# One two-layer decoder step on one core: value stores on another queue, quarter sums and pooling sums spread over the stages, projections interleaved

## The chip, the cores and the metric

One NeuronCore of a Trainium2 chip; the other cores are idle. The metric is the device time of one launch in microseconds. A core has TensorE (matmuls, PE in the profile; PEld is its weight load), VectorE (DVE), ScalarE (ACT), GpSimd (POOL) and SyncE (SP), which here only issues DMAs. Each engine runs its own instructions in the order in which they were issued to it, and waits at its head for whatever that instruction needs. Matmul results land in PSUM, all other tiles are in SBUF, inputs and outputs in HBM.

## What is computed

A trunk of two layers over 1024 prompt tokens and 8 sample tokens, 1024 features, float32. Cut to what matters here:

```python
h = x @ w_in[l]                       # columns: pooling, gating MLP, queries, keys, values, gates
q, k = rope(q), rope(k)               # 8 query heads, 2 key heads of 64
ya = pool_mix(xa) * silu(za)          # causal means over 2, 4, 8, 16 tokens
vn = layer_norm(v_sgu, sg, sb)        # the gating MLP's values, normalised
yb = u * sgu_spatial(vn) * silu(zb)
yc = window_attention(q, k, v, sinks) * silu(zc)
y  = sum(sigmoid(g_i) * (y_i @ w_proj_i) for i in (a, b, c))
x  = layer_norm(ALPHA * x + y @ w_out[l])
```

Key, value, pooling and gating states are outputs too.

## The kernel before

**Arithmetic.** A float32 product is three matmuls on a faster input type: each operand is split into a high and a low half (`split`, L96: a ScalarE copy L97 makes the high half, a subtraction L98 the low half, on VectorE unless GpSimd is named), and h*xh + h*xl + lo*xh is summed in PSUM. The input x lies transposed in SBUF as XH and XL, 8 tiles of 128 features by 1032 tokens; HT = 516 tokens are half of it.

**Weights** come in through SyncE's queue in the order of `order()` into six raw buffers `wr` (L92). The list `todo` holds the preparations in that order; `prep()` runs the next one, which splits one half tile of weights (512 columns) into `wh` and `wl` (four buffers each), puts it on the list `ready` and issues further loads.

**Stages of a layer**, the times of the first layer in brackets:

- Values (`a0`, 0 to 60): nine blocks of tokens, 24 matmuls each over values and gating values. `a0_post` (L347) copies the values on ScalarE, and normalises the gating values: statistics on VectorE, a power on GpSimd (L304), subtract and multiply on VectorE (L357), then scale and bias as two GpSimd operations (L358, L359). The stores of these rows are issued on ScalarE's queue, one block late.
- Rotation (`rope`, 60 to 120): five column tiles (keys, four of queries) of three units (matmuls L607). Each unit copies four quarters on ScalarE (L387), multiplies on VectorE (L388, L389) and adds on GpSimd (L390). After the keys a job `keys_out` transposes the last ones (L398) for the output, eight pumps later.
- Gates (`gates`, 120 to 450, twelve calls of `pair`, L847): a pair computes 2 x 2 quarter results with seven products (`product`, L832, matmuls L839) of sums of weights with sums of input quarters, like Strassen's. VectorE adds a product to the results (L855, L865), which frees its PSUM buffers. Sums of weights are made on GpSimd (L209 to L217), quarter sums of the input (`S`, L672 to L702) and their splits (`P`, into T2x, T3x, T4x) by jobs during the value and rotation stages (`queue_folds`). Attention runs as jobs in between: `att_scores` (L457), `att_norm` (L479), transposes (L496), weighted sums.
- Pooling branch (450 to 500): `pool_sums` (L749) doubles running sums on GpSimd, further jobs widen them on VectorE (L772).
- Gating MLP, then the last gated branch `gate_c` (to 569), whose result is finished by L917 to L919. The branches' results are split as yh, yl by `split_y` and `split_c`, four of these eight low halves on GpSimd.
- Projections (`project(d)`, from 569, matmuls L964): for each of eight column tiles d three groups i (pooling and gating MLP: two feature tiles each; attention: four). VectorE multiplies each half group by its gate out of PSUM (L969); gates were stored to HBM and are loaded again (L942).
- Output projection, layer norm and transposes (to 772), then the second layer, whose value and rotation stage lies at 772 to 890.

**Jobs.** Class `Jobs` keeps four lists. Stages call `pump()`: one call is one tick, and runs the jobs whose conditions hold. A condition is a pair (event, lag): the job may start that many ticks after the event. Of list 3, the quarter sums, one job at most starts per pump. `need(event)` runs whatever is missing for an event at once.

PSUM has eight buffers: four `acc` (value, rotation, products, half of the projections) and four `att`.

Of the kernel before, what the change touches and what calls it, by code (L numbers as in the profile page):

```python
# [18 lines left out]
S = 1024  # L19
# [82 lines left out]
def trunk_kernel(  # L102
# [69 lines left out]
    def order():  # L172
        for l in range(L):
# [160 lines left out]
    class Layer:  # L334
        def __init__(self, l):
            self.l, self.c, self.jobs = l, LC[l], Jobs()
            self.s, self.pt, self.res, self.rr, self.row, self.y = [{} for _ in range(6)]
            self.late, self.step, self.vn_out = deque(), 0, None
# [8 lines left out]
        def a0_post(self, b, p):  # L347
# [9 lines left out]
            V.tensor_scalar(vn_dst[:n], p[:n, 128:384], mv[:n, 0:1], mv[:n, 1:2], op0=ALU.subtract, op1=ALU.mult)  # L357
            G.tensor_tensor(vn_dst[:n], vn_dst[:n], c["sg"][:n], op=ALU.mult)  # L358
            G.tensor_tensor(vn_dst[:n], vn_dst[:n], c["sb"][:n], op=ALU.add)  # L359
            if self.vn_out:  # L360
                self.vn_out()
                self.vn_out = None
            if b < NB:
                self.vn_out = lambda: A.dma_start(out=vnd[:, b], in_=vn_dst)
            if b == NB - 1:
                A.dma_start(out=vp_o[l], in_=v_dst)
            elif b == NB:
                A.dma_start(out=vs_o[l, :, 127, :], in_=self.vs)
                A.dma_start(out=cv_o[l], in_=vn_dst[:NS])
                A.dma_start(out=vnsd, in_=vn_dst[:NS])  # L370
# [86 lines left out]
        def att_scores(self, q):  # L457
# [3 lines left out]
            st, nm, su = self.s[q] = (t_ap()[:, 0:512], *self.two(t_sm(4, "ns")))  # L461
# [14 lines left out]
            V.tensor_tensor(nm, nm, self.c["sk"][:, j:j + 2], op=ALU.add)  # L476
            A.activation(nm, nm, AF.Exp)
# [198 lines left out]
        def queue_folds(self):  # L676
# [32 lines left out]
            prev = [("x", 1)]  # L709
# [6 lines left out]
            def P_(n, k, *at):  # L716
                nonlocal prev
                J.add(3, lambda: parts(n, k), ("TT", n, k), prev + list(at))
                prev = [(("TT", n, k), 1)]
# [29 lines left out]
        def pool_sums(self, j):  # L749
# [4 lines left out]
            G.tensor_tensor(X[:, 1:S], x[:, 1:S], x[:, 0:S - 1], op=ALU.add)  # L754
            G.tensor_copy(X[:, 0:1], x[:, 0:1])
# [6 lines left out]
            self.jobs.mark(("sum", j))  # L762
            nxt, J = Y if cur is X else X, self.jobs
# [68 lines left out]
        def product(self, n, ps, first):  # L832
            h, lo = ready.popleft()
            for k in range(4):
# [9 lines left out]
                if k in (0, 2) and len(ready) < 3:  # L844
                    prep()
# [87 lines left out]
        def open_gates(self):  # L933
            self.g = {}

        def load_gate(self, i, d, q):
            if d < 8:
                n = i or d % 2 * 3
                if n not in self.g:
                    self.g[n] = t_u(("u4", "u5", "u6", "u7")[n], [T], F32, "gl")  # L940
                e = slice(q * HT, q * HT + HT)
                SP.dma_start(out=self.g[n][:, e], in_=gd[i][d][:, e])  # L942
# [6 lines left out]
        def project(self, d):  # L949
            w = ready.popleft(), ready.popleft()  # L950
            m = self.g[d % 2 * 3]
            last = d == 7
            for i in range(3):
                t = self.g[i] if i else m
# [354 lines left out]
```

## Time and profile before

| | before |
|---|---|
| median of 3 runs | 1545.0 us (1543.7 to 1545.22) |
| the profiled execution, its own time | 1546.7 us |
| its span, first to last instruction | 1545.0 us |
| mean granted clock of TensorE | 0.979 of full speed |
| busy: TensorE, VectorE | 1468.7 us (95%), 1035.1 us (67%) |
| busy: ScalarE, GpSimd | 611.4 us (40%), 540.0 us (35%) |
| DMA, mean over the span | 98 GB/s |

Busy time counts computing instructions only. Rows of a timeline give the start, the duration, the engine, the line of the kernel and its tiles, and in brackets how long the engine stood idle before and what ended it.

### The profile page before, as it was taken

How to read it: one execution, taken by the hardware profiler on the slowest of the kernel's cores; microseconds unless marked ns; L12 is line 12 of the kernel's file. 1: busy time of each engine (PE TensorE's matmuls, PEld its weight loads, DVE VectorE, ACT ScalarE, POOL GpSimd, SP SyncE). 2: the span in 40 equal slices, each digit the busy share in tenths (PEclk: the TensorE clock that was granted, in tenths of full speed). 3: DMA queues.
4: the chain of work that ended last, by engine and by line, in shares of the span. 5: the costliest groups of instructions: out<-in, count | busy, mean ns of one | idle time of the engine just before them, and what ended most of it. 6: DMA issues, size and time to landing. Idle time of an engine off the chain costs nothing. (4 is left out here: it accounts for less than half of the span.)

```text
span 1545.0 us, 27806 instructions
## 1 busy us (share of the span) xinstructions
PE 1468.7 (95%) x10592; PEld 1379.1 (89%) x10592; DVE 1035.1 (67%) x2262; ACT 611.4 (40%) x1419; POOL 540.0 (35%) x520
## 2 busy tenths in 40 slices
PE   8898999999999999999997989999999999899998
PEld 8788999999999989988796989999999999899886
DVE  6785666666558686654888756666766586866547
ACT  4365555565532242220213645655555332422200
POOL 4534322332143124510574443232312422245015
PEclk9999999999999998999998999999999999999999
DMA  7312222222222125642323121222222221256413
GB/s 250 109 43 68 71 83 83 77 89 76 90 80 73 49 76 173 210 144 93 136 75 119 51 69 63 97 69 84 82 84 83 88 71 46 85 186 205 132 49 123
DMA packets 82388, 151.92 MB, mean 98 GB/s; under 512 B 13216, under 2 KB 22512, under 8 KB 82224
## 3 DMA queue, kind: packets, MB, share of 16 engines
q1 hardware_dynamic: 62928, 113.65, 23.7%
q10 hardware_dynamic: 19328, 36.51, 6.2%
q8 instruction: 83, 1.36, 0.4%
q14 instruction: 49, 0.40, 0.1%
HBM read 113.62 MB, written 38.58 MB: 99 GB/s over the span
## 5 line engine op out<-in xcount | busy, mean ns | idle before, releaser
L839 PE MATMUL acc<-XH,wh 128*128 128x258 f32 x1152 | 235.9, 286 | 3.9 <-ACT gu L865 3.4
L839 PE MATMUL acc<-XL,wh 128*128 128x258 f32 x1152 | 235.4, 286 | 0.0
L839 PE MATMUL acc<-XH,wl 128*128 128x258 f32 x1152 | 235.2, 285 | 0.0
L98 DVE TENSOR_TENSOR wl<-wr,wh 128x512 fp32r<-128x512 f32 x196 | 155.2, 792 | 94.8 <-ACT wh L97 90.7
L839 PEld LDWEIGHTS acc<-XH,wh 128*128 128x128 f32 x1152 | 178.9, 189 | 9.8 <-issue 4.2
L839 PEld LDWEIGHTS acc<-XH,wl 128*128 128x128 f32 x1152 | 178.7, 189 | 5.5 <-issue 5.0
L839 PEld LDWEIGHTS acc<-XL,wh 128*128 128x128 f32 x1152 | 178.6, 189 | 4.7 <-issue 4.2
L97 ACT ACTIVATE wh<-wr 128x512 fp32r<-128x512 f32 x196 | 122.1, 624 | 131.9 <-PE acc L839 42.5
L210 POOL TENSOR_TENSOR st<-st,wr 128x512 f32<-128x512 f32 x36 | 51.5, 1430 | 287.2 <-DVE wl L98 244.5
L98 DVE TENSOR_TENSOR wl<-st,wh 128x512 fp32r<-128x512 f32 x108 | 85.2, 789 | 68.6 <-ACT wh L97 67.1
L315 PE MATMUL acc<-slx,XH 128*128 128x512 f32 (+1 forms) x384 | 113.4, 377 | 0.4 <-DVE slx L98 0.4
L839 PE MATMUL acc<-T2x,wh 128*128 128x258 f32 x576 | 101.6, 294 | 10.8 <-DVE gu L855 10.8
L971 POOL TENSOR_TENSOR glu<-glu,glu 128x516 f32<-128x516 f32 x56 | 80.5, 1449 | 83.1 <-DVE glu L969 45.1
L474 ACT ACTIVATE ap<-ap,ns 128x256 f32<-128x256 f32 (+1 forms) x128 | 62.4, 488 | 113.1 <-DVE ns L472 113.1
L855 DVE TENSOR_TENSOR gu<-gu,acc 128x258 f32<-128x258 f32 x240 | 90.0, 416 | 18.4 <-PE acc L839 18.4
L839 PE MATMUL acc<-T4x,wh 128*128 128x258 f32 x576 | 99.0, 294 | 3.3 <-DVE zyu L855 3.3
L905 ACT ACTIVATE gu<-gu,halves 128x258 f32<-128x258 f32 x144 | 65.7, 504 | 90.8 <-DVE gu L855 89.2
L839 PE MATMUL acc<-T3x,wh 128*128 128x258 f32 x576 | 98.1, 288 | 0.9 <-DVE gu L855 0.9
L839 PEld LDWEIGHTS acc<-T2x,wh 128*128 128x128 f32 x576 | 83.3, 194 | 16.2 <-issue 9.9
L217 POOL TENSOR_TENSOR st<-wr,st 128x512 f32<-128x512 f32 x36 | 48.3, 1342 | 130.9 <-issue 127.8
L607 PE MATMUL acc<-XH,wh 128*128 128x384 f32 (+1 forms) x240 | 80.8, 337 | 10.6 <-DVE kTu L388 5.5
L209 POOL TENSOR_TENSOR st<-wr 128x512 f32<-128x512 f32 x36 | 47.2, 1312 | 123.6 <-DVE wl L98 88.5
(252 smaller groups left out, 3583.0 us busy)
## 6 DMA issues: line engine op xcount, KB each, us to landing
wr<-in_wS_dram SPq DMA_DIRECT2D x144, 256.0 KB, 2.6
gd<-gu ACTq DMA_DIRECT2D x48, 516.0 KB, 2.7
glu<-gd SPq DMA_DIRECT2D x96, 258.0 KB, 2.7
wr<-in_wP_dram SPq DMA_DIRECT2D x32, 256.0 KB
wr<-in_wO_dram SPq DMA_DIRECT2D x32, 256.0 KB, 3.4
wr<-in_wB_dram SPq DMA_DIRECT2D x20, 256.0 KB, 2.7
w<-in_xp_dram SPq DMA_DIRECT2D x16, 256.0 KB
w<-x2d SPq DMA_DIRECT2D x16, 256.0 KB, 2.6
```

Of the source, the lines that this page charges most:

```text
L97: nc.scalar.activation(h, raw, AF.Copy)
L98: (eng or nc.vector).tensor_tensor(lo, raw, h.bitcast(F32), op=ALU.subtract)
L209: G.tensor_tensor(s1[:, 0:512], a21, a22, op=ALU.add)
L210: G.tensor_tensor(s2[:, 0:512], s1[:, 0:512], a11, op=ALU.subtract)
L217: G.tensor_tensor(s4[:, 0:512], a12, sums[p][1], op=ALU.subtract)
L315: PE.matmul(p[:, 0:n], x[:, k, blk(b)], c, start=(i == 0 and j == 0), stop=(i == len(terms) - 1 and j == len(t) - 1))
L474: A.activation(o, o, AF.Exp, bias=nm[:, i:i + 1], scale=-1.0, accum_out=su[:, i:i + 1])
L607: PE.matmul(p[:, 0:n], a[:, c], b[:, k, o:o + n], start=(k == 0 and j == 0), stop=(k == 7 and j == 2))
L839: PE.matmul(ps[s][:, 0:258], a[:, c], b[:, s * 258:s * 258 + 258], start=(first and k == 0 and j == 0), stop=(k == 3 and j == 2), skip_gro ...
L855: V.tensor_tensor(part(c, q, s), part(*a, s), b[s][:, 0:258], op=ALU.add)
L905: A.activation(o, p, AF.Tanh, bias=self.c["h"][:, i * 8 + d + c:i * 8 + d + c + 1], scale=0.5)
L971: (V if last else G).tensor_tensor(m[:, e], m[:, e], t[:, e], op=ALU.add)
```

## The change

1. `order()`: the weight halves of the first two projection tiles come by half, not by tile.
2. `a0_post`: normalise, scale and bias as two VectorE operations, none on GpSimd; the stores of these rows are issued on SyncE's queue, at the next block (`send`).
3. `keys_out` 16 pumps after the keys, not 8.
4. `att_scores`: the sink term of the softmax gets a result tile of its own (`sn`), where it overwrote the negative maximum.
5. `queue_folds`: other lags between the quarter sums. The last split P(4,3) moves in the first layer from tick 80 to 91, in the second from 65 to 78, of 96.
6. `pool_sums`: the doublings are jobs of list 3, four pumps apart, where they were issued in one go.
7. `product`: the two weight preparations come after matmul groups 1 and 5, ahead of the pumps at 3 and 7, where they came at the end of tiles 0 and 2.
8. `project`: the first two column tiles are interleaved (pooling of both, gating MLP of both, then attention of both); gates are loaded by this order; the splits of yc go between the first groups, and all low halves are VectorE's.
9. `split_x`, first layer: the low halves of input blocks 3, 5 and 7 on GpSimd.

```diff
 order():
-            for d in range(8):
+            yield from [wP[l, d, :, h * 512:h * 512 + 512] for h in range(2) for d in range(2)]
+            for d in range(2, 8):
 a0_post():
-            V.tensor_scalar(vn_dst[:n], p[:n, 128:384], mv[:n, 0:1], mv[:n, 1:2], op0=ALU.subtract, op1=ALU.mult)
-            G.tensor_tensor(vn_dst[:n], vn_dst[:n], c["sg"][:n], op=ALU.mult)
-            G.tensor_tensor(vn_dst[:n], vn_dst[:n], c["sb"][:n], op=ALU.add)
-            if self.vn_out:
-                self.vn_out()
+            V.scalar_tensor_tensor(vn, p[:n, 128:384], mv[:n, 0:1], c["sg"][:n], op0=ALU.subtract, op1=ALU.mult)
+            V.scalar_tensor_tensor(vn, vn, mv[:n, 1:2], c["sb"][:n], op0=ALU.mult, op1=ALU.add)
+            self.send()
...
+        def send(self):
+            for dst, src in self.out:
+                SP.dma_start(out=dst, in_=src)
+            self.out = []
 rope():
+                if s == 1:
+                    self.send()
-                self.jobs.add(0, self.keys_out, None, [("k", 8)])
+                self.jobs.add(0, self.keys_out, None, [("k", 16)])
 att_scores():
-            V.tensor_tensor(nm, nm, self.c["sk"][:, j:j + 2], op=ALU.add)
-            A.activation(nm, nm, AF.Exp)
+            V.tensor_tensor(sn, nm, self.c["sk"][:, j:j + 2], op=ALU.add)
+            A.activation(sn, sn, AF.Exp)
 queue_folds():
+            prev, gap = [("x", 1)], 1 + self.l
-                prev = [(("TT", n, k), 1)]
+                prev = [(("TT", n, k), gap)]
-            S_(2, 0, 3, ("wA", 1))
+            S_(2, 0, 3, ("wA", 2))
+            lag = 4 - self.l
-                S_(4, k, 2)
+                S_(4, k, lag)
-                    S_(2, k + 1, 3)
+                    S_(2, k + 1, lag)
 pool_sums():
+            def double(a, b, sh):
+                G.tensor_tensor(b[:, sh:S], a[:, sh:S], a[:, 0:S - sh], op=ALU.add)
+                G.tensor_copy(b[:, 0:sh], a[:, 0:sh])
+                return False
...
-                G.tensor_tensor(nxt[:, sh:S], cur[:, sh:S], cur[:, 0:S - sh], op=ALU.add)
-                G.tensor_copy(nxt[:, 0:sh], cur[:, 0:sh])
+                J.add(3, lambda a=cur, b=nxt, sh=sh: double(a, b, sh), ("ps", j, i + 1), [(("ps", j, i), 4)])
...
-                      [(("wide", j, 0), 2) if i else (("sum", j), (6, 16)[j])])
+                      [(("wide", j, 0), 2) if i else (("sum", j), 3)])
 product():
-                if k in (0, 2) and len(ready) < 3:
-                    prep()
+                    elif k * 3 + j in (1, 5) and len(ready) < 3:
+                        prep()
 open_gates(), project():
+            steps = [(0, 0), (1, 0), (0, 1), (1, 1), (2, 0), (2, 1)]
+            self.steps = steps + [(i, d) for d in range(2, 8) for i in range(3)]
+            rest = [x for x in self.steps if x[0]]
+            self.slot = {x: 1 + n % 2 for n, x in enumerate(rest)}
...
+            for x, (i, d) in enumerate(self.steps):
+                if i == 0 or i == 2:
+                    w = ready.popleft()
+                if x < 3:
+                    self.split_c((1, 3, 2)[x])
 split_x():
-        split(nc, XH[:, ks, blk(b)], XL[:, ks, blk(b)], xraw[b][:, ks])
+        split(nc, XH[:, ks, blk(b)], XL[:, ks, blk(b)], xraw[b][:, ks], G if b in (3, 5, 7) else V)
 main:
-        y.gate_c(2, {2: lambda: y.split_y(0), 21: lambda: y.split_y(1, G), 3: lambda: y.split_y(2),
-                     1: lambda: y.split_y(3, G), 4: lambda: (y.split_c(0), y.split_c(1, G))})
-        y.split_c(3, G)
-        y.split_c(2)
+        y.gate_c(2, {2: lambda: y.split_y(0), 21: lambda: y.split_y(1), 3: lambda: y.split_y(2),
+                     1: lambda: y.split_y(3), 4: lambda: y.split_c(0)})
-        for d in range(8):
-            y.project(d)
+        y.project()
```

## Rows read from the trace of the kernel before

**Rows 1.** The page, busy time of each engine (us, share of the span, instructions).

```profile
PE 1468.7 (95%) x10592; PEld 1379.1 (89%) x10592; DVE 1035.1 (67%) x2262; ACT 611.4 (40%) x1419; POOL 540.0 (35%) x520
```

**Rows 2.** Stretches: length, busy time PE, PEld, DVE, ACT, POOL, PEclk, DMA share, GB/s.

```profile
45.00:118.00 73.00, 62.09 (x364) 60.05 (x363) 59.43 (x88) 38.80 (x80) 33.31 (x28) 0.93 0.23 68
104.80:111.00 6.20, 4.37 (x16) 3.62 (x15) 3.70 (x8) 5.16 (x11) 0.97 (x1) 0.72 0.14 42
450.00:500.00 50.00, 48.13 (x365) 46.31 (x364) 40.02 (x73) 13.71 (x30) 22.47 (x19) 0.97 0.23 58
565.00:600.00 35.00, 28.19 (x202) 27.20 (x202) 27.15 (x48) 11.65 (x19) 16.40 (x9) 0.85 0.39 126
785.00:890.00 105.00, 93.95 (x556) 91.03 (x556) 80.05 (x129) 45.36 (x97) 56.27 (x54) 0.95 0.24 75
```

**Rows 3.** Waits of TensorE: us in total, times, longest.

```profile
PE acc L839 <- DVE gu L855: 11.7, 21, 1.1
...
PE att L398 <- POOL kTu L390: 8.3, 2, 4.9
```

**Rows 4.** Timelines, first layer: start, us, operation, tiles, [idle before <- releaser].

```profile
48.39 0.55 DVE L357 TENSOR_SCALAR w<-acc,sv 128x256 f32<-128x256 f32 x1 [2.33 <-POOL sv L304]
...
61.94 1.96 ACT L387 ACTIVATE w<-acc 32x384 f32<-32x384 f32 x4 [5.89 <-DMA out_dram<-vs]
...
63.93 0.56 DVE L388 TENSOR_TENSOR kTu<-acc,tabu 128x384 f32<-128x384 f32 x1 [3.44 <-ACT w L387]
```

**Rows 5.** Timelines of VectorE, GpSimd and TensorE into the projections, first layer.

```profile
557.87 0.42 DVE L918 SCALAR_TENSOR_TENSOR zu<-w,acc 128x258 f32<-128x258 f32 x1 [0.87 <-ACT w L917]
...
559.14 2.69 POOL L98 TENSOR_TENSOR yhx<-zyu,yhx 128x1032 fp32r<-128x1032 f32 x1 [16.17 <-ACT yhx L97]
...
559.62 2.76 DVE L98 TENSOR_TENSOR wl<-st,wh 128x512 fp32r<-128x512 f32 x1
562.30 0.74 DVE L855 TENSOR_TENSOR zu<-zu,acc 128x258 f32<-128x258 f32 x2
562.97 1.22 DVE L98 TENSOR_TENSOR yhx<-zyu,yhx 128x1032 fp32r<-128x1032 f32 x1
...
568.88 0.65 PE L964 MATMUL att<-yhx,wh 128*128 128x258 f32 x4
...
569.62 0.64 PE L964 MATMUL att<-yhx,wh 128*128 128x258 f32 x4
```

**Rows 6.** Timelines of VectorE and TensorE at the start of the first layer.

```profile
19.20 0.54 DVE L357 TENSOR_SCALAR w<-acc,sv 128x256 f32<-128x256 f32 x1 [0.67 <-POOL sv L304]
...
19.88 2.35 DVE L98 TENSOR_TENSOR XL<-xx,XH 128x1024 fp32r<-128x1024 f32 x2
...
21.72 0.33 PE L315 MATMUL acc<-slp,XL 128*128 128x384 f32 x1
```

**Rows 7.** Groups by line, 785 to 836 us, of GpSimd and VectorE.

```profile
L358 POOL TENSOR_TENSOR w<-w,lrow 128x256 f32<-128x256 f32 (+1 forms) x9 | 9.3, 1033 | 5.8 <-DVE w L357 5.8
L359 POOL TENSOR_TENSOR w<-w,lrow 128x256 f32<-128x256 f32 (+1 forms) x9 | 8.6, 958 | 0.7
...
L357 DVE TENSOR_SCALAR w<-acc,sv 128x256 f32<-128x256 f32 x8 | 4.3, 544 | 7.6 <-POOL sv L304 7.6
```

**Rows 8.** Timeline of VectorE in the second layer's rotation stage.

```profile
836.09 0.70 DVE L98 TENSOR_TENSOR T3x<-st,T3x 128x516 fp32r<-128x516 f32 x1 [1.98 <-ACT T3x L97]
```

**Rows 9.** Timelines of VectorE and ScalarE at one attention score job.

```profile
205.09 0.16 DVE L476 TENSOR_TENSOR ns<-ns,lrow 128x2 f32<-128x2 f32 x1 [0.76 <-ACT ap L474]
...
205.28 0.20 ACT L477 ACTIVATE ns<-ns 128x2 f32<-128x2 f32 x1 [0.23 <-DVE ns L476]
...
206.04 0.69 DVE L98 TENSOR_TENSOR wl<-wr,wh 128x512 fp32r<-128x512 f32 x1 [0.79 <-ACT wh L97]
```

**Rows 10.** Timeline of VectorE in the pooling stage, first layer.

```profile
463.49 2.38 DVE L772 SCALAR_TENSOR_TENSOR pxyu<-pxyu,cb 128x512 f32<-128x512 f32 x1
```

**Rows 11.** Waits of SyncE's queue: us in total, times, longest.

```profile
SPq L92 <- DMA vnd<-w: 8.5, 3, 5.2
```

More of the change, by code (lines that the diff above doesn't have):

```diff
@@ L337, in __init__ @@
             self.s, self.pt, self.res, self.rr, self.row, self.y = [{} for _ in range(6)]
-            self.late, self.step, self.vn_out = deque(), 0, None
+            self.late, self.step, self.out = deque(), 0, []
             self.jobs.pace = 2.8
@@ L460, in att_scores @@
             w = 256 if n else 128
-            st, nm, su = self.s[q] = (t_ap()[:, 0:512], *self.two(t_sm(4, "ns")))
+            st, n6 = t_ap()[:, 0:512], t_sm(6, "ns")
+            (nm, su), sn = self.two(n6), n6[:, 4:6]
+            self.s[q] = st, sn, su
             ps = t_att()
@@ L753, in pool_sums, with first @@
             X, Y = [t_u(f"u{4 + 6 * j + i}", [T], F32, "pxy") for i in range(2)]
-            G.tensor_tensor(X[:, 1:S], x[:, 1:S], x[:, 0:S - 1], op=ALU.add)
-            G.tensor_copy(X[:, 0:1], x[:, 0:1])
+            tiles, n, J = [X, Y], 0, self.jobs
+            def first():
+                G.tensor_tensor(X[:, 1:S], x[:, 1:S], x[:, 0:S - 1], op=ALU.add)
+                G.tensor_copy(X[:, 0:1], x[:, 0:1])
+                return False
+            def double(a, b, sh):
+                G.tensor_tensor(b[:, sh:S], a[:, sh:S], a[:, 0:S - sh], op=ALU.add)
+                G.tensor_copy(b[:, 0:sh], a[:, 0:sh])
+                return False
+            J.add(3, first, ("ps", j, 0), [(("sum", 0), 2)] if j else ())
             cur, sh = X, 2
@@ L933, in open_gates, with gate @@
         def open_gates(self):
-            self.g = {}
+            steps = [(0, 0), (1, 0), (0, 1), (1, 1), (2, 0), (2, 1)]
+            self.steps = steps + [(i, d) for d in range(2, 8) for i in range(3)]
+            rest = [x for x in self.steps if x[0]]
+            self.slot = {x: 1 + n % 2 for n, x in enumerate(rest)}
+            self.next = dict(zip(rest, rest[2:]))
+            self.g = {}
+        def gate(self, i, d):
+            n = self.slot[i, d] if i else d % 2 * 3
+            if n not in self.g:
+                self.g[n] = t_u(("u4", "u5", "u6", "u7")[n], [T], F32, "gl")
+            return self.g[n]
         def load_gate(self, i, d, q):
             if d < 8:
-                n = i or d % 2 * 3
-                if n not in self.g:
-                    self.g[n] = t_u(("u4", "u5", "u6", "u7")[n], [T], F32, "gl")
                 e = slice(q * HT, q * HT + HT)
-                SP.dma_start(out=self.g[n][:, e], in_=gd[i][d][:, e])
+                SP.dma_start(out=self.gate(i, d)[:, e], in_=gd[i][d][:, e])
         def merged(self, d, q, m):
@@ L947, in merged, with project @@
             self.load_gate(0, d + 2, q)
[L949 to L954, printed above, removed]
+        def project(self):
+            for x, (i, d) in enumerate(self.steps):
+                last = d == 7
+                if i == 0 or i == 2:
+                    w = ready.popleft()
+                m, t = self.gate(0, d), self.gate(i, d)
                 ks = ((0, 1), (2, 3), (4, 5, 6, 7))[i]
+                if x < 3:
+                    self.split_c((1, 3, 2)[x])
                 for q in range(2):
@@ L976, in project @@
                     if i == 2:
[L977 removed]
+                        self.late.append((self.step + 1, lambda d=d, q=q, m=m[:, e]: self.merged(d, q, m)))
                     if (i < 2 and q) or (i == 2 and not q and d >= 3):
                         prep()
[L980 removed]
+                if x == 0:
                     for q in range(2):
@@ L985, in project @@
                     cur["w0"].prep(4)
-            if last:
-                while self.late:
-                    self.late.popleft()[1]()
-                stack_sample()
+            while self.late:
+                self.late.popleft()[1]()
+            stack_sample()
         def d_load(self, b, h):
```

34 lines of the change are left out of this document (15 added, 19 removed).

## The prediction

> **What bounds the kernel now.** I read the page first, then TensorE by stretches, then what it waits for, and last the timelines of the engines that it waits for. TensorE is busy for 1468.7 of 1545.0 us [rows 1]: only its idle time, and its time at the lower clock, can be won. The table by stretches shows where both lie: in each row idle time is length minus PE busy, and the loss to the clock is about busy time times (1 - PEclk) [rows 2]. First layer, the stage of keys, values and queries (45 to 118): 10.9 idle + 62.1 x 0.07 = 4.3, together 15.3 us. Its like in the second layer (785 to 890): 11.0 + 4.7 = 15.7. Pooling (450 to 500): 1.9 + 1.4 = 3.3, twice. From the last gated branch into the projections (565 to 600): 6.8 + 4.2 = 11.0, twice. PEclk is the mean of two levels, 2.4 and 1.2 GHz; each of these stretches is under 1.00 and holds stalls of some microseconds, and one of them is the row from 104.8: 1.8 idle, and behind it 6.2 x 0.28 = 1.7 lost to the clock.
>
> The waits name VectorE and, behind it, GpSimd: the additions that empty PSUM for the gate products (L855, 11.7 us in 21 waits) and the rotated keys (L390, 8.3 in two) [rows 3]. So TensorE isn't short of weights from HBM. VectorE takes its queue in order and is late at five places; the question for each edit is whether it gets there sooner.
>
> **A. Value stage and rotation, first layer.** ScalarE issued the value stores itself. The last of them waited for earlier work, so ScalarE idled 5.89 us before the copies of the first rotated unit (L387) at 61.94, and VectorE 3.44 us before L388 at 63.93 [rows 4]; TensorE waited for that PSUM buffer. With the stores on SyncE and L358/L359 gone, nothing on ScalarE's queue holds these copies, so I let the 3.4 go whole (0 if another holder appears). VectorE's wait of 2.33 us for GpSimd before L357 at 48.39 [rows 4] falls to the usual 0.67 [rows 6]: 1.7. GpSimd's two operations of about 1.0 us each [rows 7] on the last three blocks (6 us) no longer hold VectorE up; I take 2.5 of it, between 0 and 6. Added: a second scalar_tensor_tensor on three blocks, 0.42 by its nearest row (258 columns) [rows 5], -1.3. The first one replaces a tensor_scalar of 0.55 on the same columns [rows 4]: between 0.42 and 0.55, nothing.
>
> The low halves of input blocks 3, 5, 7 move to GpSimd, and block 3's costs something. VectorE starts it at 19.88 today, and TensorE reads the first of it at 21.72 [rows 6]. If GpSimd starts then too and takes 2.69, as its split of 1032 columns does [rows 5], it is ready at 22.6: a stall of 0.9. Bounds: 0, if GpSimd starts earlier, and 2.1, if VectorE's own split of block 4 (1.2, half of the 2.35 [rows 6]) goes first. Such a pair meets at 559: a VectorE split of 512 columns takes 2.76 us beside GpSimd's 2.69 [rows 5], against 0.69 alone [rows 9]. The Trainium skill's page "SBUF — State Buffer" (SBUF: two separate sides) says that a GpSimd operation and a VectorE operation with two SBUF inputs lock each other out of a shared port for the whole instruction, whichever starts first. The trace agrees; by that rule this edit alone can lose 0.9 or 2.1 and gains nothing. Blocks 5 and 7 are read later than they can be late: nothing.
>
> Sum up to the third rotation: 3.4 + 1.7 + 2.5 - 1.3 - 0.9 = 5.4. Behind it the quarter sums are spread: the last pair moves from pump 80 to 91 of a stage that ends at 96, VectorE's load per unit falls, and the stall at 104.8 goes with its clock, 1.8 + 1.7 = 3.5 [rows 2]. Against that: a new low clock stretch of 1.7 at even odds, -0.8; the late sums keep a buffer that GpSimd's first weight sums need, -0.9 (one operation, as above). 5.4 + 3.5 - 1.7 = 7.2: **A = 7** (3 to 15.3, all that the stretch loses).
>
> **B. The same in the second layer.** VectorE's savings up to its third rotation: waits for GpSimd's power, 7.6 over 8 less 8 x 0.67, 2.3 [rows 7]; idle because ScalarE was held, 2.0 at 836.09 [rows 8]; a quarter of the 17.9 us that L358 and L359 run [rows 7], 4.4 (0 to 9, half); less 9 x 0.42 = 3.8; and the sums S(2,2), S(4,2) and splits P(4,1), P(2,2), due before pump 57 and now behind it: six operations of 516 columns, 0.70 each [rows 8] less 0.07 by which neighbours overlap (562.30 and 562.97 [rows 5]), 3.8. Together 8.7. Key output at pump 64 instead of 56 comes two units later, when the keys are done; its stall of 4.9 [rows 3] is inside that sum, because VectorE is the bound there and TensorE would only wait at the next place. **B = 8.5** (5 to 15.7).
>
> **C. Gate products.** 11.7 us in 21 waits [rows 3]. About eight are near the longest, 1.1. In the one at 206, L476 waits 0.76 us for the exponentials, then the weight split at 206.04 waits 0.79 for ScalarE, which sits behind its second exponential (itself 0.23 late, waiting for L476); only then L855 frees TensorE [rows 9]. With a separate result L476 goes before the exponentials end, but the split still waits for ScalarE: only the 0.23 is won, 1.8 for eight. The other thirteen share some 3.4 us; those without a split between lose up to 0.76 each: I take 2.5 of 3.4. The reordered weight splits do nothing in the steady state: three entries are ready when a product ends and one is used, so the first slot refills and the second finds three. **C = 4.3** (1 to 10).
>
> **D. Pooling sums.** GpSimd has the same operations, now at pumps 1, 4, 8, 12. VectorE's operations that they stretch (2.38 us for 512 columns at 463.49 [rows 10]) win only the gaps between the pumps, 1 to 2 us, but the idle time is 1.9 in all and the clock's 1.4 hangs on it [rows 2]. Taken as 2 of the 3.3 in each layer: **D = 4** (0 to 6.6).
>
> **E. Into the projections.** Four low halves leave GpSimd. While one runs there, VectorE stands (2.76 for 0.69: 2.1 lost); on VectorE it costs 1.22 [rows 5]. From 557.87 on, VectorE's queue to the first eviction of the projection is then: four times four L918/L919 at 0.43 (6.9), five splits of 1.22 (6.1), four weight splits of 0.69 (2.8), four L855 pairs of 0.74 (3.0) [rows 5, 9], 0.9 once for the hop to ScalarE [rows 5], less 0.07 at about ten joints: 19.0, so 576.9. TensorE needs that buffer after four half-groups: six matmuls take 569.62 - 568.88 = 0.74 [rows 5], twelve 1.5, so at 568.9 + 5.9 = 574.8, since the two groups in front need only the split y tiles. Stall 2.1, and 0.6 more in the next two; today 6.8 idle [rows 2]. A low clock stretch of 1.7 after it at 2 in 5: 0.7. So 11.0 - 3.4 = 7.6 a layer. A lookahead weight split now waits for a buffer of a later group, with evictions behind it in VectorE's queue; they have the next group's four half-groups as cover, and 0.7 a split without it. **E = 15.2** (7 to 22).
>
> **Sum.** 7 + 8.5 + 4.3 + 4 + 15.2 = 39. The profiled execution took 1546.7 us for a span of 1545.0; the runs' median is 1545.0, 0.1% under it. 1545.0 - 39 = **1506**.
>
> **Rivals.** (1) VectorE stays the bound, and each stall comes back at the next buffer. For it: it is busy 59.4 of 73 us in 45 to 118 [rows 2] and gets more instructions. Against: 5.89 and 3.44 us of idle time there are ScalarE's holds [rows 4]. Then A and B give 8 together, C 1, D 0, E 10: 19, 1526. (2) All listed losses go, the clock with them, because VectorE's relief is larger than I allow (6 and 9 of contention): 15.3 + 15.7 + 10 + 6.6 + 22 = 70, 1475. (3) Slower: the value stores, nine a layer, stand on SyncE's queue in front of the weight loads. One load has waited 5.2 us for such a store [rows 11]; 18 x 5.2 = 94 us of queue. Six raw buffers cover it; it decides when more than 42 of these 94 us get through to TensorE, 39 for the gain and 3 more: 1548 and over. Against: a store is sent one block after its data, when they are ready. (4) The edits hardly act: under 3 us, if VectorE's queue is refilled as far as it was shortened: 1543.
>
> Chances: my forecast 0.58, (1) 0.22, (2) 0.12, (3) 0.05, (4) 0.03. The range goes 19 below the forecast, over half way to (2), and to just past (1): 1487 to 1530, which leaves out most of (2) and all of (3) and (4), under 2 in 10. 0.2% (3 us) is what a measurement of this kernel can tell from none: faster 0.92, same 0.03, slower 0.05.
>
> **What would show it.** After: ScalarE without a hold ahead of the first L387; the wait L398 <- L390 gone; a wait of TensorE for a weight split in the third rotation (rival 2: none); one for block 3 near 22 us; waits on L855 down by a third; no GpSimd split near the projections, one wait of about 2 us there; mean granted clock near 0.99 (0.979 now). The prediction fails if VectorE is busy as long as before in the rotation stage, if GpSimd's block split costs much more than 2.1 us, or if SyncE's loads land late.

## The result, and the profile after

The changed kernel takes 1500.1 us (median of 4 runs, 1497.5 to 1501.1) against 1545.1: ratio 0.971, 95% interval 0.969 to 0.972, so 45 us faster. 1506 was predicted, 1487 to 1530. The profiled execution has a span of 1499.4 us and a mean granted clock of 0.990. The page's busy times, which answer to [rows 1]:

```profile
PE 1450.1 (97%) x10592; PEld 1365.9 (91%) x10592; DVE 1033.7 (69%) x2285; ACT 602.6 (40%) x1419; POOL 491.7 (33%) x479
```

TensorE is idle for 27.0 us less and computes 18.6 us less at the same number of matmuls: those at half clock and those behind a wait are the longer ones, and by the mean granted clock (0.979 and 0.990) the half clock cost some 32 us before and 15 after, an estimate. VectorE, with 23 instructions more, is busy for as long as before, and GpSimd for 48 us less. The stretches of [rows 2], moved to where the same work now lies (length, busy time of PE, PEld, DVE, ACT, POOL, PEclk, DMA share, GB/s):

```profile
47.80:112.20 64.40, 59.30 (x363) 58.69 (x363) 61.62 (x91) 37.05 (x77) 24.34 (x20) 0.95 0.28 87
...
438.00:488.00 50.00, 48.20 (x377) 46.19 (x375) 40.06 (x76) 14.21 (x32) 23.36 (x19) 1.00 0.24 68
552.20:587.20 35.00, 32.86 (x256) 32.34 (x255) 27.14 (x53) 12.49 (x21) 11.45 (x8) 0.95 0.45 144
764.00:861.00 97.00, 93.32 (x569) 90.61 (x568) 83.48 (x141) 45.21 (x97) 39.68 (x37) 0.98 0.25 81
```

The rotation of the first layer (47.8 to 112.2) still loses 5.1 us of idle time and 3.0 to the clock; the second layer's stage (764 to 861) 3.7 and 1.9, where it was 11.0 and 4.7. Pooling (438 to 488) loses 1.8 and nothing, where it was 1.9 and 1.4. The way into the projections (552 to 587) loses 2.1 and 1.6, where it was 6.8 and 4.2. By the start of the first or last matmul of a stage in the two timelines (of the last gate store, where the gates end), the 45.6 us of span come from here:

| stretch | before | after | gain | predicted |
|---|---|---|---|---|
| values, rotation, layer 1 | 0 to 118.0 | 0 to 112.2 | 5.8 | A 7 |
| gates, layer 1 | 118.0 to 435.7 | 112.2 to 424.4 | 5.5 | C 4.3, both layers |
| pooling, MLP, layer 1 | 435.7 to 568.9 | 424.4 to 556.1 | 1.5 | D 4, both layers |
| projections, layer 1 | 568.9 to 672.6 | 556.1 to 653.4 | 6.4 | E 15.2, both layers |
| output, then values, rotation, layer 2 | 672.6 to 887.0 | 653.4 to 857.8 | 10.0 | B 8.5 |
| gates, layer 2 | 887.0 to 1204.5 | 857.8 to 1165.6 | 9.7 | in C |
| pooling, MLP, layer 2 | 1204.5 to 1337.5 | 1165.6 to 1298.4 | 0.2 | in D |
| projections, layer 2 | 1337.5 to 1440.9 | 1298.4 to 1395.3 | 6.5 | in E |

The gates gave 15.2 in place of 4.3; all else gave 30 in place of 35. Within the first row the values take 2.8 us longer than before (the rotation starts at 47.8, not at 45.0) and the rotation 8.6 less. The waits of TensorE after the change (total, times, longest):

```profile
PE acc L613 <- DVE wl L98: 6.2, 3, 4.1
...
PE acc L856 <- ACT gu L882: 5.1, 2, 3.7
PE att L502 <- DVE ap L492: 4.2, 4, 1.9
PE att L991 <- ACT wh L97: 3.5, 2, 1.9
PE acc L856 <- DVE gu L872: 2.9, 8, 0.4
...
PE acc L316 <- POOL XL L98: 2.1, 1, 2.1
```

The additions behind the products, 11.7 us in 21 waits [rows 3], are down to 2.9 in 8 (L872). The wait behind GpSimd's rotated keys, 8.3 us in two, is gone, and the one behind VectorE's rotated keys (5.5 in two before) is down to 1.0. The weight split (L98 before L613) has grown from 2.1 in three, the longest 1.0; input block 3 (GpSimd's split before L316) is new. Both were forecast. Timelines of the first layer show them (start, us, operation, [idle before <- releaser]):

```profile
19.57 2.41 POOL L293 TENSOR_SCALAR_AFFINE_SELECT lcol<-lcol 128x128 f32<-128x128 f32 x4
21.96 2.35 POOL L98 TENSOR_TENSOR XL<-xx,XH 128x1024 fp32r<-128x1024 f32 x1
...
24.36 0.44 PE L316 MATMUL acc<-slp,XL 128*128 128x384 f32 x1 [2.06 <-POOL XL L98]
...
58.21 0.31 ACT L352 ACTIVATE vs<-w 8x128 f32<-8x128 f32 x1 [7.73 <-DVE w L328]
58.42 1.95 ACT L391 ACTIVATE w<-acc 32x384 f32<-32x384 f32 x4
...
74.91 0.70 DVE L704 TENSOR_TENSOR st<-st,XL 128x516 f32<-128x516 f32 x1
75.52 0.69 DVE L98 TENSOR_TENSOR wl<-wr,wh 128x512 fp32r<-128x512 f32 x1
...
76.26 0.69 PE L613 MATMUL acc<-XH,wl 128*128 128x384 f32 x1 [4.08 <-DVE wl L98]
```

At 21.96 GpSimd starts block 3's low half, behind its four selects, and TensorE stands 2.06 us: the 0.9 of the prediction was too little. Its upper bound of 2.1 holds in number only, as it was worked out from a split of VectorE going first. At 58.21 ScalarE has waited 7.73 us for VectorE (L328), as it had in the kernel before (9.24), but no store follows: the first rotated copies come at once, at 58.42. At 75.52 VectorE reaches the weight split of the third rotation, with quarter sums in front of it, and TensorE has waited 4.08 us for it. The wait is as long with the old lags of the quarter sums (4.1, below).

### The profile page after: what moved, and what is told of

It reads as the page before. It is cut to its first block, busy times and chain, and to the rows that moved or that the text cites. A ratio compares the mean times of both kernels' runs of the same rounds, so it can differ in the third digit from the quotient of the medians.

```text
span 1499.4 us, 27765 instructions
## 1 busy us (share of the span) xinstructions
PE 1450.1 (97%) x10592; PEld 1365.9 (91%) x10592; DVE 1033.7 (69%) x2285; ACT 602.6 (40%) x1419; POOL 491.7 (33%) x479
## 5 line engine op out<-in xcount | busy, mean ns | idle before, releaser
L856 PE MATMUL acc<-XH,wh 128*128 128x258 f32 x1152 | 236.5, 286 | 7.4 <-ACT gu L882 5.1
L98 DVE TENSOR_TENSOR wl<-wr,wh 128x512 fp32r<-128x512 f32 x196 | 153.4, 782 | 124.4 <-ACT wh L97 123.6
L856 PE MATMUL acc<-XL,wh 128*128 128x258 f32 x1152 | 236.0, 286 | 0.0
L856 PE MATMUL acc<-XH,wl 128*128 128x258 f32 x1152 | 235.7, 286 | 0.0
L856 PEld LDWEIGHTS acc<-XH,wh 128*128 128x128 f32 x1152 | 179.4, 190 | 13.5 <-ACT gu L882 5.5
L856 PEld LDWEIGHTS acc<-XH,wl 128*128 128x128 f32 x1152 | 179.1, 190 | 5.5 <-issue 5.0
L856 PEld LDWEIGHTS acc<-XL,wh 128*128 128x128 f32 x1152 | 179.3, 190 | 4.7 <-issue 4.2
L97 ACT ACTIVATE wh<-wr 128x512 fp32r<-128x512 f32 x196 | 122.3, 624 | 122.4 <-PE acc L856 44.3
L98 DVE TENSOR_TENSOR wl<-st,wh 128x512 fp32r<-128x512 f32 x108 | 78.0, 723 | 69.0 <-ACT wh L97 67.7
L316 PE MATMUL acc<-slx,XH 128*128 128x512 f32 (+1 forms) x384 | 113.6, 378 | 0.4 <-DVE slx L98 0.4
L872 DVE TENSOR_TENSOR gu<-gu,acc 128x258 f32<-128x258 f32 x240 | 89.9, 415 | 25.1 <-PE acc L856 24.9
L856 PE MATMUL acc<-T2x,wh 128*128 128x258 f32 x576 | 99.1, 290 | 3.4 <-DVE gu L872 2.9
L856 PE MATMUL acc<-T4x,wh 128*128 128x258 f32 x576 | 95.3, 286 | 1.8 <-DVE zyu L872 1.8
L856 PE MATMUL acc<-T3x,wh 128*128 128x258 f32 x576 | 96.2, 286 | 0.0
L856 PEld LDWEIGHTS acc<-T2x,wh 128*128 128x128 f32 x576 | 81.8, 192 | 6.7 <-issue 4.5
L613 PE MATMUL acc<-XH,wl 128*128 128x384 f32 (+1 forms) x240 | 78.6, 328 | 6.2 <-DVE wl L98 6.2
```

The costliest lines, as they stand in the source:

```text
L97: nc.scalar.activation(h, raw, AF.Copy)
L98: (eng or nc.vector).tensor_tensor(lo, raw, h.bitcast(F32), op=ALU.subtract)
L316: PE.matmul(p[:, 0:n], x[:, k, blk(b)], c, start=(i == 0 and j == 0), stop=(i == len(terms) - 1 and j == len(t) - 1))
L613: PE.matmul(p[:, 0:n], a[:, c], b[:, k, o:o + n], start=(k == 0 and j == 0), stop=(k == 7 and j == 2))
L856: PE.matmul(ps[s][:, 0:258], a[:, c], b[:, s * 258:s * 258 + 258], start=(first and k == 0 and j == 0), stop=(k == 3 and j == 2), skip_gro ...
L872: V.tensor_tensor(part(c, q, s), part(*a, s), b[s][:, 0:258], op=ALU.add)
```

## The experiments

All were timed in 4 runs beside 7 of the kernel before. The medians of the latter went from 1545.3 to 1547.8 us, against 1545.1 beside the kernel after, so that differences against 1500.1 can hold up to 2.7 us that are not the edit's. By the ratios the first five in the table are 19.6, 9.0, 6.3, 4.2 and 0.8 us, and only the first three have an interval apart from that of the kernel after. For the others the stages of the profiles decide; the projections of all runs that leave them alone agree within 0.3 us. Line numbers are each kernel's own and shift by a few: the product's matmul is L856 or L854 (L841 with the kernel before as base), its addition L872, L870 or L857. First, parts undone in the kernel after:

| undone | median, us | against after | ratio to before, interval |
|---|---|---|---|
| 4, sink term's own tile | 1521.6 | +21.5 | 0.983 (0.982 to 0.985) |
| 8, the order of the groups, with 1 | 1509.6 | +9.5 | 0.977 (0.975 to 0.978) |
| 2, GpSimd's scale and bias | 1509.5 | +9.4 | 0.975 (0.973 to 0.977) |
| 5, lags of the quarter sums | 1505.4 | +5.2 | 0.973 (0.972 to 0.975) |
| 8, the engine of four low halves | 1503.7 | +3.5 | 0.971 (0.969 to 0.973) |
| 6, pooling sums | 1501.4 | +1.2 | 0.970 (0.968 to 0.972) |
| 2, the queue of the stores | 1501.1 | +0.9 | 0.971 (0.969 to 0.973) |
| 7, place of the weight preparations | 1500.6 | +0.5 | 0.970 (0.968 to 0.971) |
| 9, input splits on GpSimd | 1497.6 | -2.5 | 0.968 (0.967 to 0.970) |

**The sink term.**

```diff
-            V.tensor_tensor(sn, nm, self.c["sk"][:, j:j + 2], op=ALU.add)
-            A.activation(sn, sn, AF.Exp)
+            V.tensor_tensor(nm, nm, self.c["sk"][:, j:j + 2], op=ALU.add)
+            A.activation(nm, nm, AF.Exp)
```

> The kernel after, with the sink term of the softmax written over the negative maximum again (part 4 undone); the rest as changed. The gates took 15 us less after (first layer 5.5, second 9.7 between the first product and the last gate store), where the prediction gave them 4.3. Theory 1, the separate tile did it: VectorE no longer stops for the exponentials, so the weight split and the additions behind it come earlier by the whole 0.6 us a wait, and the stalls before the transposes shrink too: about 1512, the waits on the additions (L872 here) back from 2.9 to about 10 us. Theory 2, the other order of weight preparation did it: 1500, waits as after. As the prediction priced it, 0.23 us in eight waits and 2.5 in the others: 1504.

The separate tile is two further columns of the tile `ns`. 1521.6 us: theory 1, and by more than it said. The gates of the two layers are 11.2 and 10.7 us longer. Its waits:

```profile
PE acc L854 <- DVE gu L870: 12.1, 22, 1.1
PE att L500 <- DVE ap L490: 8.4, 4, 3.4
```

Both are back where they were before the change. VectorE's timeline around the same wait, without and then with the separate tile:

```profile
199.91 0.74 DVE L870 TENSOR_TENSOR gu<-gu,acc 128x258 f32<-128x258 f32 x2
...
204.22 0.16 DVE L480 TENSOR_TENSOR ns<-ns,lrow 128x2 f32<-128x2 f32 x1 [0.76 <-ACT ap L478]
205.17 0.69 DVE L98 TENSOR_TENSOR wl<-wr,wh 128x512 fp32r<-128x512 f32 x1 [0.79 <-ACT wh L97]
205.78 0.42 DVE L870 TENSOR_TENSOR gu<-gu,acc 128x258 f32<-128x258 f32 x1
...
206.35 0.87 PE L854 MATMUL acc<-T2x,wh 128*128 128x258 f32 x4 [1.11 <-DVE gu L870]
```

```profile
195.76 0.75 DVE L872 TENSOR_TENSOR gu<-gu,acc 128x258 f32<-128x258 f32 x2
...
199.36 0.16 DVE L482 TENSOR_TENSOR ns<-ns,lrow 128x2 f32<-128x2 f32 x1
200.70 0.69 DVE L98 TENSOR_TENSOR wl<-wr,wh 128x512 fp32r<-128x512 f32 x1 [1.18 <-ACT wh L97]
201.31 0.75 DVE L872 TENSOR_TENSOR gu<-gu,acc 128x258 f32<-128x258 f32 x2
...
201.87 0.87 PE L856 MATMUL acc<-T2x,wh 128*128 128x258 f32 x4 [0.31 <-DVE gu L872]
```

Without the separate tile, from the addition one product earlier (199.91) to the one that frees TensorE (205.78) takes 5.87 us; with it 5.55 (195.76 to 201.31). So 0.32 is won in this product, near the 0.23 of the prediction. But TensorE's wait falls from 1.11 to 0.31: the other half microsecond was won further ahead, since the earlier addition too comes sooner against TensorE. VectorE had carried its lag on from earlier products. How much VectorE itself won shows in its own waits, without and then with the separate tile:

```profile
DVE wl L98 <- ACT wh L97: 164.8, 118, 4.3
DVE ns L480 <- ACT ap L478: 49.0, 64, 1.3
```

```profile
DVE wl L98 <- ACT wh L97: 191.3, 145, 4.3
```

The wait for the exponentials, 49.0 us in 64 jobs, is gone, and 26.5 of it come back as waits of weight splits for ScalarE. The 22.5 that stay won are about what the kernel wins: some 0.35 us a job, close to the 0.32 of this one, but in every job and not only in those at which TensorE is seen to wait. That is an estimate from the sums; the 64 jobs were not followed one by one. In the two layers' gates TensorE's idle time is 13.4 us longer without the tile, near the 13.4 by which the two listed waits grow; the other 8.3 are longer matmuls, at half clock and behind waits (the four at 201.87 take 0.87 us, four in a row 0.65 [rows 5]).

The same edit alone, in the kernel before:

> The kernel before, with part 4 alone: the sink term of the softmax gets a tile of its own. Undone in the kernel after it cost 21.5 us. Theory: it works by itself, because the waits for the exponentials lie in the gates of both layers and nothing else of the change touches those: 1523 to 1526, waits on the additions (L855's line) from 11.7 to about 3 us, stalls before the transposes from 8.4 to about 4. Rival: part of it needs the other edits, which start the gates with less VectorE work left over: 1530 or more.

1526.1 us, ratio 0.986 (0.984 to 0.989): 21 us by itself, at the upper edge of the theory's 1523 to 1526. Its waits at the same two places:

```profile
PE att L498 <- DVE ap L488: 4.1, 4, 1.9
...
PE acc L841 <- DVE gu L857: 3.0, 8, 0.6
```

**The weight preparations of a product.**

```diff
-                    elif k * 3 + j in (1, 5) and len(ready) < 3:
-                        prep()
+                if k in (0, 2) and len(ready) < 3:
+                    prep()
```

> The kernel after, with the two weight preparations of a product back at the ends of tiles 0 and 2 (part 7 undone). The prediction says this part does nothing, since the first slot always refills: 1500, and waits on the additions at 2.9 us as after. Theory 2, it puts ScalarE's weight copy ahead of the jobs of a pump and that is what shortened the waits: 1508 to 1512, and waits of 0.9 to 1.1 us back before the products on T2x.

1500.6 us, all stages within 1 us of the kernel after: it does nothing, as predicted.

**The pooling sums**, issued in one go again:

```diff
-                J.add(3, lambda a=cur, b=nxt, sh=sh: double(a, b, sh), ("ps", j, i + 1), [(("ps", j, i), 4)])
+                G.tensor_tensor(nxt[:, sh:S], cur[:, sh:S], cur[:, 0:S - sh], op=ALU.add)
+                G.tensor_copy(nxt[:, 0:sh], cur[:, 0:sh])
```

> The kernel after, with the doublings of the pooling sums issued in one go again (part 6 undone). As predicted: 4 us for both layers, 1504, a wait of 1.6 us before the product on T4x and a low clock stretch behind it in each layer. By the difference of the two profiles between the last gate store and the first projection (1.5 and 0.2 us): 1502.

1501.4 us. The wait before the product on T4x is back, 1.63 us in place of 0.90, in both layers, but no low clock stretch follows it in either, and the stage is 1.3 and 0.1 us longer. With the doublings as jobs the first wait of the stage is the longer one, 0.71 us in place of 0.24, so that part of the gain is lost again. And the stage of the first layer is 1.1 us longer in the run with the input splits on VectorE too, which leaves the pooling alone. The part is worth about 1 us, which the runs can't tell from nothing.

**The projections: the engine of the splits.**

```diff
-                    self.split_c((1, 3, 2)[x])
+                    self.split_c((1, 3, 2)[x], (G, G, V)[x])
...
-        y.split_y(1) ... y.split_y(3)
+        y.split_y(1, G) ... y.split_y(3, G)
```

> The kernel after, with four low halves on the way into the projections on GpSimd again; the projection groups stay interleaved. Theory: it is the engine, each GpSimd split holds VectorE for 2.1 us, so most of the 12.9 us that the projections gained goes: 1508 or more, waits of 2 to 3 us before the first projection groups and low clock stretches. Rival: it is the order of the groups, which gives VectorE time: 1503 at most.

1503.7 us, the projections 2.2 and 2.5 us longer: between the two, nearer to the rival. By the medians alone this part is not told from nothing; the projections of the profile show it.

**The projections: the order of the groups.**

```diff
-            steps = [(0, 0), (1, 0), (0, 1), (1, 1), (2, 0), (2, 1)]
+            steps = [(0, 0), (1, 0), (2, 0), (0, 1), (1, 1), (2, 1)]
```

The order of the weight halves and of the gate loads goes back with it.

> The kernel after, with the projection groups of the first two column tiles in their old order (pooling, gating MLP and attention of tile 0, then of tile 1); the low halves stay on VectorE. With the splits back on GpSimd only 4.4 of the 12.9 us that the projections had gained were lost. Theory: the other 8 come from the order, which gives VectorE two more half groups of each kind before the attention groups need yc: 1507 to 1509, a wait of 3 us or more before the third group of each layer with a low clock stretch. Rival: either edit alone is enough, so undoing one costs as little as undoing the other: 1502 to 1504.

1509.6 us, the projections 6.0 and 5.2 longer. VectorE and TensorE where the attention group now comes third:

```profile
568.57 2.30 DVE L98 TENSOR_TENSOR yclu<-yc,ychx 128x1032 fp32r<-128x1032 f32 x1
...
570.92 0.80 PE L991 MATMUL att<-yclu,wh 128*128 128x258 f32 x2 [5.37 <-DVE yclu L98]
```

TensorE waits 5.37 us for the split of yc, which VectorE finishes at 570.9. It is the same queue of splits as in the kernel after; there the groups of the second tile cover it.

**The values: scale and bias on GpSimd again**, stores on SyncE.

```diff
-            V.scalar_tensor_tensor(vn, p[:n, 128:384], mv[:n, 0:1], c["sg"][:n], op0=ALU.subtract, op1=ALU.mult)
-            V.scalar_tensor_tensor(vn, vn, mv[:n, 1:2], c["sb"][:n], op0=ALU.mult, op1=ALU.add)
+            V.tensor_scalar(vn, p[:n, 128:384], mv[:n, 0:1], mv[:n, 1:2], op0=ALU.subtract, op1=ALU.mult)
+            G.tensor_tensor(vn, vn, c["sg"][:n], op=ALU.mult)
+            G.tensor_tensor(vn, vn, c["sb"][:n], op=ALU.add)
```

> The kernel after, with scale and bias of the normalised values as two GpSimd operations again (half of part 2 undone); the stores stay on SyncE. The stores alone, put back on ScalarE, cost nothing that could be measured. Theory: the rows that are finished late by GpSimd were the cause of what ScalarE's hold cost, and GpSimd's operations stretch VectorE's, so this half carries all of part 2: 1505 to 1510, the rotations of both layers later by 2 to 5 us each. Rival: neither half alone is worth anything, as either removes the hold: 1499 to 1502.

1509.5 us, the span of the profile 8.8 longer. The rotation of the first layer starts 4.0 us later and takes 1.1 more; that of the second starts another 3.3 later and takes 0.7 more. GpSimd and TensorE:

```profile
19.67 1.87 POOL L360 TENSOR_TENSOR w<-w,lrow 128x256 f32<-128x256 f32 x1 [0.66 <-DVE w L359]
21.61 0.73 POOL L361 TENSOR_TENSOR w<-w,lrow 128x256 f32<-128x256 f32 x1
22.30 1.03 POOL L293 TENSOR_SCALAR_AFFINE_SELECT lcol<-lcol 128x128 f32<-128x128 f32 x4
23.29 2.34 POOL L98 TENSOR_TENSOR XL<-xx,XH 128x1024 fp32r<-128x1024 f32 x1
...
25.68 0.69 PE L316 MATMUL acc<-slp,XL 128*128 128x384 f32 x1 [3.97 <-POOL XL L98]
...
804.10 0.66 PE L614 MATMUL acc<-XH,wh 128*128 128x384 f32 x1 [3.37 <-DVE w L359]
```

Block 3's split stands behind scale, bias and selects, so its wait is 3.97 us here, not 2.06, and TensorE's granted clock is 0.51 from 24.8 to 31.8 us, where it is 1.00 in the kernel after. So in the first layer most of the loss comes of GpSimd having both these operations and the input splits of part 9; scale and bias on GpSimd without part 9 were not tried. The hold of ScalarE is gone in this run too: its copies follow the sample values at once, and TensorE's waits for rotated keys are 1.3 us in two. The second layer's rotation starts 3.37 us late, behind the normalisation (L359), as in the kernel before (3.4 behind L357).

**The stores on ScalarE's queue again**, normalisation on VectorE.

```diff
-                SP.dma_start(out=dst, in_=src)
+                A.dma_start(out=dst, in_=src)
```

> The kernel after, with the value stores on ScalarE's queue again, still one block late, normalisation on VectorE (half of part 2 undone). Theory: a store only held ScalarE because it waited for GpSimd's L359 and an earlier store; with the rows finished on VectorE a store one block late finds its data ready: at most 1 us slower, 1500 to 1501. As the prediction priced it (3.4 us in the first layer and 2.0 in the second belong to ScalarE's hold): 1505.

1501.1 us: the theory. With the rows finished on VectorE the queue makes no difference that shows. So either half alone removes ScalarE's hold, stores on SyncE or rows that are ready; what the hold was worth no run shows, as the two halves were not undone together.

**Input splits on VectorE.**

```diff
-G if b in (3, 5, 7) else V
+V
```

> The kernel after, with all low halves of the input blocks on VectorE again (part 9 undone). The prediction says that this part alone can only lose: the wait of 2.1 us for block 3 at 22 us goes and nothing comes in its place: 1498, and the rotation starts 2 us earlier. Rival: VectorE has no room in the value stage, now that it normalises alone, and is later at the rotation by the 3 x 1.2 us of these splits: 1500 to 1504.

1497.6 us, ratio 0.968 (0.967 to 0.970); the rotation starts 1.8 us earlier and is no longer than in the kernel after. Beside the kernel after the intervals overlap, the profile shows the wait gone. So part 9 only costs, as the prediction said of it by itself.

**The old lags of the quarter sums.**

```diff
-            prev, gap = [("x", 1)], 1 + self.l
+            prev, gap = [("x", 1)], 1
...
-                S_(4, k, lag)
+                S_(4, k, 2)
...
-                    S_(2, k + 1, lag)
+                    S_(2, k + 1, 3)
```

> The kernel after, with the old lags of the quarter sums (part 5 undone). As the prediction has it, the spread sums free VectorE late in the rotation (3.5 us in the first layer, 3.8 in the second) and delay GpSimd's first weight sums: 1503 to 1506, waits for weight halves in the last two rotations back, and ScalarE's wait for GpSimd before the gates (3.7 us of TensorE in the first layer) shorter. Rival: what the spread wins in the rotation it loses again at that place: 1499 to 1501.

1505.4 us. The rotations are 3.0 and 2.4 us longer, the first layer's gates 2.2 shorter. Its waits:

```profile
PE acc L613 <- DVE wl L98: 9.3, 5, 4.1
...
PE acc L856 <- ACT gu L882: 4.1, 2, 2.7
...
PE acc L613 <- ACT wh L97: 1.8, 1, 1.8
```

The weight split costs 9.3 us in place of 6.2, the stall of 1.8 on ScalarE's half is back, and the wait at the start of the gates (L882) is 2.7, not 3.7: the spread sums win in the rotation and give part of it back there.

**A better version.** Three edits on the kernel after: the input splits, the rotation's addition, and an early clearing.

```diff
-                G.tensor_tensor(dst, dst, t[:, 0:n], op=ALU.add)
+                V.tensor_tensor(dst, dst, t[:, 0:n], op=ALU.add)
...
         def open_p(self):
+            smp = t_u("u8", [960], F32, "smp")
+            self.qz, self.ss = smp[:, 0:576], smp[:, 576:960]
+            G.memset(self.qz, 0.0)
```

> The kernel after, with three more edits: the low halves of the input blocks on VectorE (1497.6 by itself), the addition of the rotation (L394) on VectorE instead of GpSimd, and the clearing of the sample queries' tile ahead of the rotation. VectorE's operations in the rotation of the first layer are stretched by 14 us beside GpSimd, in the second by 8, most of it by this addition (15 and 16 us of GpSimd); on VectorE 15 additions cost about 7 us a layer. Theory: the stretching is worth more than the additions cost, and ScalarE no longer waits for GpSimd before the gates (3.7 us of TensorE and a low clock stretch): 1490 to 1494. Rival: VectorE is the bound there and gets 7 us more to do: 1500 to 1506.

1494.6 us, ratio 0.966 (0.963 to 0.968), just over the theory's range. Busy times in the rotation, with the input splits alone and then with all three:

```profile
45.00:112.00 67.00, 61.87 (x385) 60.97 (x384) 64.05 (x93) 38.78 (x81) 26.07 (x22) 0.95 0.28 86
```

```profile
45.00:112.00 67.00, 62.17 (x382) 61.60 (x381) 63.17 (x107) 39.98 (x84) 11.74 (x11) 0.95 0.27 84
```

VectorE has 14 instructions more and is busy 0.9 us less: the additions cost what the stretching had cost, so the rotation itself is no shorter. Most of the gain over the input splits alone lies in the first layer's gates (4.0 us), at whose start ScalarE no longer waits for GpSimd. Which of the two further edits did it, the addition or the early clearing, was not separated:

```profile
PE acc L856 <- ACT gu L882: 1.4, 2, 1.0
```

**And the weight preparation ahead of a rotation unit's matmuls:**

```diff
-                p, e, n = self.unit(w, s)
                 if s < 2 and len(ready) < 2:
                     prep()
+                p, e, n = self.unit(w, s)
```

> The kernel of the run before (input splits and the rotation's addition on VectorE, tile cleared early) with the weight preparation of a rotation unit ahead of its matmuls and the quarter sums of their pumps, not behind. TensorE waits 4.1 us in the third rotation of the first layer and 1.8 in the second for a weight split, in every kernel of this study with the new lags, and each wait has a low clock stretch behind it (6.9 and 3.4 us at half clock, 3.4 and 1.7 lost). The split moves ahead of five VectorE operations of 0.69 us, 3.4 us. Theory: the wait is a matter of order in VectorE's queue: 0.7 and 0 us are left of it, the clock stretches go, 1484 to 1489. Rival: VectorE is the bound there, and the wait comes back at the next PSUM buffer, the multiplication L392: 1492 to 1496.

1488.3 us, ratio 0.962 (0.960 to 0.963), the fastest version of this study and within the theory's range, but not by its mechanism alone. TensorE in the third rotation:

```profile
70.39 0.44 PE L613 MATMUL acc<-XH,wl 128*128 128x384 f32 x1 [0.73 <-DVE wl L98]
...
75.92 0.59 PE L613 MATMUL acc<-XH,wl 128*128 128x384 f32 x1 [3.17 <-DVE wl L98]
```

The wait for the first half is 0.73, as worked out, but the second half's now takes 3.17: in the first layer the rival is right in the main, and the rotation gains 1.0 us. In the second layer the wait goes and the rotation gains 2.6, of which the gates give 1.6 back. The two profiles differ by 2.7 us in span, the medians by 6.3; how much of the latter is this edit stays open.

## Why the prediction was right, and where it was not

**What bounds it.** Right: TensorE's idle time and its longer matmuls, at half clock and behind waits, are what was won, and VectorE's lag is what each part with a gain acts on. The sum came near, 45 for 39, by errors of both signs (under the rivals).

**A, 7 predicted, 5.8 measured, and less than that.** The wait at the third rotation, the one for block 3 and the end of ScalarE's hold came as described; with the hold TensorE's wait for the first rotated keys went, 3.9 us (5.5 in two before, 1.0 in one after), near the 3.4, though no run gives the hold's worth by itself. Undone one by one, scale and bias on VectorE are worth 5.1 here, the lags 3.0 and the input splits -2.0. Two terms were mis-sized. Block 3 took 2.06, not 0.9, as the four selects stand ahead of it. And the 0.9 for what the late sums do to the start of the gates: without the sink term's 11.2 us the first layer's gates would have lost 5.7 (4.1 against the kernel before with part 4 alone), 1.7 of it in the wait at L882 (3.7 us; the first of the two that the kernel before has there is 2.0), where ScalarE stands behind GpSimd's clearing. Of this 2.2 go when the old lags come back, and the better version, with the clearing early and the addition on VectorE, wins 4.2 there. So A and this loss together came to nearly nothing. The prediction's own sign of failing, VectorE as busy as before in the rotation stage, came too: 61.6 us of 64.4 after, 59.4 of 73 before. The stage got shorter all the same, so this sign was ill chosen.

**B, 8.5 predicted, 10.0 measured.** Right in sum. Undone one by one, scale and bias on VectorE are worth 4.0 of it and the lags 2.4. The other 3.6, with the end of ScalarE's hold and the later key output (part 3) in it, no run separates.

**C, 4.3 predicted; 15.2 measured in the gates, and 21 for part 4 by itself.** The step that failed is "only the 0.23 is won, 1.8 for eight": it followed one wait through one product, from ScalarE's exponentials to the addition, took VectorE's arrival at that job as given, and counted the eight jobs at which TensorE waits longest. Its size for one job was near (0.32 there). The runs show that the arrival moved as well, as VectorE gains some 0.35 in each of the 64 jobs (the estimate above): 21 waits became 8, the eight long ones shrank from about 1.0 to 0.36 each, and the stalls before the transposes (L502, 8.4 to 4.2), which the term left out, halved. The upper bound of 10 was made from the waits on L855 alone, and 15.2 lies outside it. That the weight preparations do nothing was right.

**D, 4 predicted, about 1 measured.** Neither step held. The wait before the product on T4x fell from 1.64 to 0.90 us, but another of the stage grew, and the idle time went from 1.9 to 1.8 only. And the clock's 1.4 a layer doesn't hang on it: with the sums put back, and in the kernel before with part 4 alone, the wait of 1.6 came without a low clock stretch.

**E, 15.2 predicted, 12.9 measured.** The one wait of about 2 us that was left is there in the first layer (1.89) and two of 1.6 and 1.5 in the second. It has the cause that was forecast, VectorE's first multiplication out of PSUM (L996):

```profile
563.46 0.75 DVE L996 SCALAR_TENSOR_TENSOR glu<-glu,att 128x258 f32<-128x258 f32 x2
...
564.02 0.86 PE L991 MATMUL att<-yhx,wh 128*128 128x258 f32 x4 [1.89 <-ACT wh L97]
```

The profile names a ScalarE copy (L97) that ended 0.07 us ahead. But the first of the two multiplications ends 0.15 ahead, as VectorE does before every wait of this kernel for the additions (L872), so TensorE most likely stood behind VectorE. The prediction gave the gain to the engine of the splits and took the order of the groups as cover for the rest; undone one at a time, the order is worth 11.2 of the projections' time and the engine 4.7 (9.5 and 3.5 by the medians).

**The rivals.** (1), VectorE stays the bound, holds for the first layer's rotation alone, where it is busy for 96% of the stage. (3), SyncE's queue, is answered: stores on either queue give the same time. That the sum came within 6 us rests on errors of both signs: part 4 was taken 17 us too small, A, with the loss at the gates, D and E together some 12 too large. Part 3, the later key output, was not tried alone.

## What to carry to other kernels

An in-place update is a wait: a result written over an input that another engine still reads stopped the busiest helper in every job, and two columns of their own were worth nearly half of this change. Where an engine with a queue in order runs late all through a stage, price a shortened job at every place where it runs (64 here), and not only at those where TensorE is seen to wait (eight): the lag is carried on. Not all of a wait that goes is won, either: of VectorE's 49 us half came back at its next wait. When a transfer seems to hold an engine, ask also who is late with its data: here either another queue or earlier data ended the hold.

## What the hardware showed

A VectorE operation that reads two SBUF operands was stretched beside a GpSimd split, one that reads PSUM and SBUF was not. Timelines of the kernel after:

```profile
23.05 0.47 DVE L359 SCALAR_TENSOR_TENSOR w<-acc,sv,lrow 128x256 f32<-128x256 f32 x1
24.85 2.62 DVE L360 SCALAR_TENSOR_TENSOR w<-w,sv,lrow 128x256 f32<-128x256 f32 x1 [1.32 <-POOL sv L305]
...
24.78 2.40 POOL L98 TENSOR_TENSOR XL<-xx,XH 128x1024 fp32r<-128x1024 f32 x1
...
30.39 0.48 DVE L360 SCALAR_TENSOR_TENSOR w<-w,sv,lrow 128x256 f32<-128x256 f32 x1 [0.34 <-POOL sv L305]
```

L360 (two SBUF tiles) takes 2.62 us beside GpSimd's split, against 0.48 with GpSimd idle (30.39); L359 (PSUM and SBUF) takes 0.47 while GpSimd runs block 3's split (21.96 to 24.31). The Trainium skill's page "SBUF — State Buffer" (SBUF: two separate sides) names two SBUF inputs as one of the cases in which VectorE and a GpSimd operation that reads SBUF keep each other off a shared port pair; the trace agrees, by these three durations.
